# A hybrid attention/retention layer in fp32 on one core: retention values projected with tokens on partitions, rotations in that group, eight heads beside the gates' group

## The chip, the core and the metric

The kernel runs on one core of a Trainium2 chip, in one launch. The metric is device microseconds of that core from launch to end, as the median of several executions. A profile is one more execution, with a time of its own. TensorE (PE in the profile, PEld for its weight loads) makes matrix products into PSUM, eight banks of 128 x 512 fp32; ScalarE (ACT) and VectorE (DVE) read PSUM and SBUF; GpSimd (POOL) reads SBUF; SyncE (SP) issues nearly all DMAs, in order, on one queue.

## The reference

One layer on `x` (1 x 1024 x 2048), fp32: an adaptive RMSNorm, one input projection to eight blocks of 1024 columns, stick-breaking attention on the first four blocks (eight heads of 128), chunkwise retention on the last four (eight heads), one output projection.

```python
mod = jax.nn.silu(c) @ w_ada[layer] + b_ada[layer]
shift, scale, gate = jnp.split(mod, 3, axis=-1)
h = rms_norm(x, norm_gain[layer]) * (1.0 + scale[:, None, :]) + shift[:, None, :]
proj = h @ w_in[layer]
q_sb, k_sb, v_sb, z_sb, q_r, k_r, v_r, z_r = jnp.split(proj, split_at, axis=-1)
...
qr = rotary(split_heads(q_r, RET_HEADS))
kr = rotary(split_heads(k_r, RET_HEADS)) * (HEAD_DIM ** -0.5)
vr = split_heads(v_r, RET_HEADS).astype(jnp.float32)
ob = head_group_norm(chunkwise_retention(qr, kr, vr), ret_norm_gain[layer])
ob = ob * jax.nn.silu(z_r.astype(jnp.float32))
y = jnp.concatenate([oa, ob], axis=-1).astype(x.dtype) @ w_out[layer]
x = x + (gate[:, None, :] * y).astype(x.dtype)
```

`rotary` turns the two halves of the 128 channels against each other: `[t1*cos - t2*sin, t1*sin + t2*cos]`. Retention goes in chunks of 128 tokens: a masked product of queries and keys times the values within a chunk, plus the decayed query times a state that each chunk updates from its keys and values.

## The kernel before

**Products.** An fp32 product is three fp32r matmuls (`mm3`, L183 to L186): each operand is cut into a high part (ScalarE, L171) and a low part (VectorE, L173), and high x high, high x low and low x high are added in PSUM. The input projection is done in groups. A group takes four pairs of 128 columns (`q` = 0 to 3) and forms them by a Strassen-like scheme of seven products (`ORDER`) in place of eight; each product has 8 entries (two halves `hh` of the contraction, four `q`), each entry 12 matmuls of 128x128 against 128x512 into the bank of its `q` (`run_entry`, L464). So a group is 56 entries, 672 matmuls. The weights are the stationary operand, the activations the moving one: the output stands with channels on partitions and tokens along the row.

**Groups.** Group 0 starts while the norm's factors are made; groups 0 to 3 hold the attention's q, k, z and v, groups 4 and 5 the retention's keys and values of four heads each (`rk`, `rv`), group 6 (`LAST`) the retention's gates. The retention's queries were made ahead and lie in `rqraw`. Then follows the output projection (`y` in the profile), 56 steps in the same scheme.

**Transfers.** `pump` (L261) keeps two supplies full, within shares of 92 slots of 128 x 512: the raw weights (`A`, 32 loads a group, rows of 512 bytes) and the *ring* of activation factors (`B11`, `T4` and so on, 112 loads a group), each asked for as slots come free. Finished halves go from `c` tiles to DRAM (`pr_rk`, `pr_rv`), by `final` in `evac` (L392).

**Order.** All engines get their instructions in the order in which the code writes them. Each entry calls `tick` twice, so a tick is six matmuls. A tick writes what `later(n, ...)` has put to it, lets one waiting task take a step, and one weight sum. Tasks are generators; what they yield is the number of ticks until their next step. The low halves of weights are cut `LOOK` = 3 entries ahead.

**Retention heads.** `ret_heads` (L1530) is such a task. It starts when head 7 of the attention is done, in group 5. For each head `ret_prepare` (L1342) loads half by half keys and queries, each with a copy whose upper and lower 64 channels are swapped (`sw`), rotates them on VectorE nine ticks later (three instructions a half, L1356 to L1361), and loads the values. `ret_attention` (L1377) then writes a head's work in four steps with `RT_GAP` = 6 ticks between: `turn_k` (transposes of the keys), `values_in` (transposes of the values, L1391 to L1396, two sets of four, each with a ScalarE copy back), `scores`, `states`, `values`, and the normalization, whose last transposes (`finish`) fall into the next head. A head's mask `dm` is loaded when the head starts. Heads 0 to 2 and the start of head 3 run in group 5, the others in group 6 and in the first eight steps of the output projection; at its step 16 all that is left of the tasks is written out (`while tasks: tick()`).

Of the kernel before, what the change touches and what calls it, by code (L numbers as in the profile page):

```python
# [11 lines left out]
F32 = mybir.dt.float32  # L12
# [5 lines left out]
P = 128  # L18
S = 1024
# [4 lines left out]
NH = 8  # L24
# [7 lines left out]
TURN = 2  # L32
RT_GAP = 6
NZ = 7
# [62 lines left out]
def layer_kernel(ctx, tc, x, c, w_ada, b_ada, norm_gain, w_in, sb_q_gain, sb_k_gain, ret_norm_gain, w_out,  # L97
# [17 lines left out]
    rqraw = [dr.tile([P, S], F32, name=f"rqraw{h}") for h in range(NH)]  # L115
    proj = {f"{n}{h}": dr.tile([P, S], F32, name=f"pr_{n}{h}") for n in ("q", "k", "z", "v", "rk", "rv")
            for h in range(NH)}
    krow = [dr.tile([1, S], F32, name=f"krow{h}") for h in range(NH)]
    sums_o = {(n, k): dr.tile([P, S], F32, name=f"sum_{n}_{k}") for n in ("T2", "T3") for k in range(8)}
# [263 lines left out]
    def evac(gi, prod, q, o):  # L383
# [79 lines left out]
    def run_entry(j):  # L463
# [11 lines left out]
        for k in range(4):  # L475
# [7 lines left out]
            if k % 2:  # L483
                tick()


# [854 lines left out]

    def ret_prepare(h):  # L1342

        r = {}

        def load(n, src, hf):
            r[n, hf] = t = get(f"r{n}_{h}_{hf}", "att")
            nc.sync.dma_start(t, src[:, halves(hf)])
# [5 lines left out]
            def rotate():  # L1354
# [6 lines left out]
                nc.vector.tensor_tensor(t, t, sw, op=ALU.add)  # L1361
                put(sw)
            later(9, rotate)

        def load_v():
            for g in range(2):
                r["v", g] = t = get(f"rv_{h}_{g}", "att")
                nc.sync.dma_start(t, proj[f"rv{h}"][:, halves(g)])

        load("k", proj[f"rk{h}"], 0)  # L1370
        later(2, lambda: load("q", rqraw[h], 0))
        later(4, load_v)
        later(6, lambda: load("k", proj[f"rk{h}"], 1))
        later(8, lambda: load("q", rqraw[h], 1))
        return r

    def ret_attention(h, r, gap):  # L1377
# [10 lines left out]
        def four(t):  # L1388
            return t.rearrange("p (j n) -> p j n", n=P)

        def values_in(g, t):  # L1391
            tp = ps.tile([P, HALF], F32, tag=next_bank(), name=f"rvt_{h}_{g}")
            for j in range(4):
                nc.tensor.transpose(tp[:, j * P:(j + 1) * P], t[:, j * P:(j + 1) * P], ident)
            v[g] = t
            later(1, lambda: nc.scalar.activation(t, tp, AF.Copy))  # L1396

# [107 lines left out]

        vr = [r["v", g] for g in range(2)]
        if unfinished:
            unfinished.pop()()
        turn_k(0)
        values_in(0, vr[0])  # L1510
        scores(0)
        yield gap
        turn_k(1)
        states(0)
        scores(1)
        yield gap
        values_in(1, vr[1])
        values(0)
# [11 lines left out]
    def ret_heads():  # L1530
        while prog.get(NH - 1, 0) < 12 or phase[0] < 5:
            yield 1
        for i, n in enumerate(("cos", "sin")):
            for hf in range(2):
                tables[n, hf] = t = get(f"{n}_{hf}", "att")
                nc.sync.dma_start(t, rot[i][:, halves(hf)])
        nxt = ret_prepare(0)
        yield 14
        while prog[NH - 1] < 99:
            yield 1  # L1540
        for h in range(NH):
            r = nxt
            for i, wait in enumerate(ret_attention(h, r, RT_GAP)):
                if i == 0 and h < NH - 1:
                    while h == 3 and phase[0] < 6:
                        yield 1
                    nxt = ret_prepare(h + 1)
# [5 lines left out]
        put(*tables.values())  # L1553

# [144 lines left out]
    for j in range(len(entries)):  # L1699
        gi, prod, hh, q = entries[j]  # L1700
        if j == 0 or entries[j - 1][0] != gi:
# [5 lines left out]
            if gi == 5:  # L1707
                start(ret_heads(), 3)
            slots.loose = gi == LAST
# [22 lines left out]
        if left_over <= 3:  # L1732
            cut_right(3 - left_over, 0)
        run_entry(j)

# [192 lines left out]
```

## Time and profile before

| | |
|---|---|
| median of 3 runs | 1884.33 us (1883.38 to 1884.34) |
| the profiled execution | 1884.66 us |
| its span, first to last instruction | 1882.9 us |
| PE busy / DVE busy / ACT busy | 1866.6 / 1341.8 / 826.1 us |
| DMA engines' mean share over the span, SyncE's queue | 86.9% |
| group 5 (retention k, v of heads 4 to 7) | 1182 to 1372 us |
| group 6 (retention gates) | 1372 to 1568 us |
| output projection | 1568 us to the end |

How to read it: a matmul's row shows 390 ns, but matmuls overlap, and what one costs is the distance from one start to the next. The share of the DMA engines is the time of all packets over the time of 16 engines; it can pass 1, since a packet's time includes what it waits for. `PEclk` is the granted clock; it is 1.00 in all windows shown.

### The profile page before, as it was taken

The page shows a single profiled execution, that of the slowest core. Times are in us where ns is not written, and L with a number is a line of the kernel's source. Part 1 is how long each engine was busy: PE and PEld are TensorE (multiplying, and loading weights), DVE is VectorE, ACT ScalarE, POOL GpSimd, SP SyncE. Part 2 cuts the span into 40 slices and gives each one's busy share as a digit, 9 for nine tenths or more (in the row PEclk, how much of TensorE's full clock was granted, in tenths as well). Part 3 has the DMA queues.
Part 4 walks back from the last instruction along what each step waited for, and adds up shares of the span by engine and source line. Part 5 has one row for each costly group of instructions (what it writes and reads, how often), then busy time and mean ns, then how long its engine had stood idle before and what let it go on. Part 6 is the DMA issues. An engine that isn't in the chain of part 4 may idle for free.

```text
span 1882.9 us, 29009 instructions
## 1 busy us (share of the span) xinstructions
PE 1866.6 (99%) x9565; PEld 1540.5 (82%) x9565; DVE 1341.8 (71%) x2601; ACT 826.1 (44%) x1559; POOL 82.6 (4%) x278
## 2 busy tenths in 40 slices
PE   8999999999999999999999999999999999999998
PEld 5777788888888888888888888888888888888887
DVE  3568776666768677877688676977585666596669
ACT  3647762233544454445443554334334455342231
POOL 0000000000110010001010101000000000000000
PEclk9999999999999999999999999999999999999999
DMA  9979999998698789978997988999997963994594
GB/s 317 361 240 313 319 348 370 374 359 300 209 315 299 242 285 310 305 272 264 321 317 263 305 276 290 302 304 290 308 317 253 265 214 113 359 366 163 187 313 164
DMA packets 414451, 541.04 MB, mean 287 GB/s; under 512 B 34142, under 2 KB 210648, under 8 KB 414300
## 3 DMA queue, kind: packets, MB, share of 16 engines
q1 hardware_dynamic: 413436, 538.78, 86.9%
q8 instruction: 75, 1.23, 0.3%
q14 instruction: 76, 0.62, 0.1%
q10 hardware_dynamic: 864, 0.40, 0.1%
HBM read 453.03 MB, written 86.02 MB: 286 GB/s over the span
## 4 chain that ended last, share of the span: by engine, by line
PE 92%; DVE 4%; DMA 3%; issue 1%; ACT 0%; SPq 0%; DVEq 0%; ACTq 0%
PE pj L184 19%; PE pj L186 19%; PE pj L185 19%; PE y L185 5%; PE y L184 5%; PE y L186 5%; PE first L184 3%; PE first L186 2%; PE first L185 2%; PE accp L569 1%; PE tp_B L1248 1%; PE oT L184 1%; PE oT L186 1%; PE oT L185 1%; DMA ada<-in_w_ada_dram 1%; PE zp L186 1%
## 5 line engine op out<-in xcount | busy, mean ns | idle before, releaser
L173 DVE TENSOR_TENSOR wl<-A,wh 128x512 fp32r<-128x512 f32 x392 | 270.1, 690 | 211.5 <-ACT wh L171 198.1
L171 ACT ACTIVATE wh<-A 128x512 fp32r<-128x512 f32 x392 | 247.6, 632 | 387.0 <-PE pj L185 369.8
L387 ACT ACTIVATE c<-pj 128x512 f32<-128x512 f32 x112 | 66.7, 600 | 147.4 <-PE pj L186 137.4
L294 DVE TENSOR_TENSOR A<-A,A 128x512 f32<-128x512 f32 x160 | 110.0, 693 | 1.7
L390 DVE TENSOR_TENSOR c<-pj,c 128x512 f32<-128x512 f32 x112 | 74.9, 687 | 47.9 <-PE pj L186 47.5
L1212 ACT ACTIVATE om<-zp,y 128x128 f32<-128x128 f32 (+2 forms) x96 | 55.9, 582 | 107.4 <-PE zp L186 67.2
L184 PE MATMUL first<-h_hi,wh_first 128*128 128x512 f32 x224 | 94.6, 422 | 0.1
L1228 DVE TENSOR_TENSOR_SCAN om<-om 128x128 f32<-128x128 f32 (+2 forms) x96 | 93.5, 974 | 1.1
L184 PE MATMUL pj<-T1h,wh 128*128 128x512 f32 x232 | 94.2, 406 | 0.0
L184 PE MATMUL pj<-B22h,wh 128*128 128x512 f32 x232 | 92.8, 400 | 0.0
L184 PE MATMUL pj<-B21h,wh 128*128 128x512 f32 x232 | 92.0, 397 | 0.0
L184 PE MATMUL pj<-B11h,wh 128*128 128x512 f32 x232 | 91.4, 394 | 0.0
L186 PE MATMUL pj<-T1h,wl 128*128 128x512 f32 x232 | 90.7, 391 | 0.0
L186 PE MATMUL pj<-B22h,wl 128*128 128x512 f32 x232 | 90.6, 391 | 0.0
L185 PE MATMUL pj<-T1l,wh 128*128 128x512 f32 x232 | 90.5, 390 | 0.0
L185 PE MATMUL pj<-B21l,wh 128*128 128x512 f32 x232 | 90.5, 390 | 0.0
L186 PE MATMUL pj<-B21h,wl 128*128 128x512 f32 x232 | 90.4, 390 | 0.0
L186 PE MATMUL pj<-B11h,wl 128*128 128x512 f32 x232 | 90.4, 390 | 0.0
L185 PE MATMUL pj<-B11l,wh 128*128 128x512 f32 x232 | 90.4, 390 | 0.0
L185 PE MATMUL pj<-B22l,wh 128*128 128x512 f32 x232 | 90.4, 390 | 0.0
L184 PE MATMUL pj<-T3h,wh 128*128 128x512 f32 x224 | 89.6, 400 | 0.0
L184 PE MATMUL pj<-T4h,wh 128*128 128x512 f32 x224 | 89.5, 400 | 0.0
(411 smaller groups left out, 4963.2 us busy)
## 6 DMA issues: line engine op xcount, KB each, us to landing
A<-in_w_in_dram SPq DMA_DIRECT2D x228, 256.0 KB, 5.7
ada<-in_w_ada_dram SPq DMA_DIRECT2D x120, 256.0 KB, 5.6
wB<-in_w_out_dram SPq DMA_DIRECT2D x112, 256.0 KB, 5.3
gr<-in_w_ada_dram SPq DMA_DIRECT2D x64, 256.0 KB, 5.6
T2h<-fac_T SPq DMA_DIRECT2D x56, 256.0 KB, 5.4
T2l<-fac_T SPq DMA_DIRECT2D x56, 256.0 KB, 5.4
T1h<-fac_T SPq DMA_DIRECT2D x56, 256.0 KB, 5.4
T1l<-fac_T SPq DMA_DIRECT2D x56, 256.0 KB, 5.3
```

The lines of the kernel that those rows point to most:

```text
L171: nc.scalar.activation(hi[:, 0:n], src[:, 0:n], AF.Copy)
L173: nc.vector.tensor_tensor(lo[:, 0:n], src[:, 0:n], hi[:, 0:n].bitcast(F32), op=ALU.subtract)
L184: nc.tensor.matmul(o, a_hi, b_hi, start=first, stop=False, skip_group_check=on)
L185: nc.tensor.matmul(o, a_hi, b_lo, start=False, stop=False, skip_group_check=on)
L186: nc.tensor.matmul(o, a_lo, b_hi, start=False, stop=last, skip_group_check=on)
L294: nc.vector.tensor_tensor(r[o], r[a], r[b], op=ALU.add if n == 1 else ALU.subtract)
L387: nc.scalar.activation(t, o, AF.Copy)
L390: nc.vector.tensor_tensor(dst[q, cc], o, dst[q, cc], op=ALU.add)
L569: nc.tensor.matmul(ap_[32 * g:32 * g + 32, :], silu_z[:, j, :], ada[cc, j // 2][:, (j % 2) * 256:(j % 2) * 256 + 256], start=j < 4, stop=j ...
L1212: nc.scalar.activation(om[:, :n], zp[:, :n], AF.Sigmoid, scale=y[:, 16 + i:17 + i])
L1228: nc.vector.tensor_tensor_scan(rev, rev, rev, init, op0=ALU.mult, op1=ALU.bypass)
L1248: nc.tensor.transpose(banks_[j // 2][:, c0:c0 + P], be[:, j * P:(j + 1) * P], ident)
```

## The change

Group 4 now holds the keys of all eight heads, and group 5 (`ACROSS`) all values, with the operands' roles turned: activations stationary, 512 columns of weights moving (`run_across`), so that tokens stand on partitions, as the head's products need them. The values go to `rvt`. `values_in` with its transposes and copies is gone; `values_in` in `ret_prepare` is now the name of two loads. A new task, `turn_in`, starts with group 5, waits for the same point of attention head 7 as `ret_heads` did, makes all 32 half-rotations, one every three ticks, and stores each to DRAM (`rot_k`, `rot_q`). `ret_heads` is started near the end of group 5, waits for group 6, and runs all heads with `RT_GAP` = 4, loading rotated halves; a guard on `turns` holds a head's loads until its halves are stored. The raw weights of group 5 are loaded as rows of 2 KB.

```diff
-RT_GAP = 6
+RT_GAP = 4
...
+    rvt = {(c_, hf): dr.tile([P, 4, HALF], F32, name=f"rvt_{c_}_{hf}") for c_ in range(2) for hf in range(2)}
+    turned_in = {(n, h): dr.tile([P, S], F32, name=f"rot_{n}{h}") for n in "kq" for h in range(NH)}
...
-    for a in (0, 4):
-        groups.append([(base + b * P, proj[f"{n}{b}"], proj[f"{n}{b + 1}"])
-                       for b in (a, a + 2) for n, base in (("rk", 5 * GW), ("rv", 6 * GW))])
+    groups.append([(5 * GW + a * P, proj[f"rk{a}"], proj[f"rk{a + 1}"]) for a in range(0, NH, 2)])
+    ACROSS = len(groups)
+    groups.append([(6 * GW, None, None)] * 4)
...
+        if gi == ACROSS:
+            kc += q
+            col = groups[gi][q][0] + (HALF if block[1] == "2" else 0)
+            nc.sync.dma_start(t, w_in[0][kc * P:(kc + 1) * P, col:col + HALF])
+            return
...
+            if gi == ACROSS:
+                def out():
+                    nc.sync.dma_start(rvt[int(cc[0]) - 1, hf][:, q, :], t)
+                    put(t)
+                later(2, out)
+                return
...
+    def run_across(j):
+        gi, prod, hh, q = entries[j]
+        prepare_sum(j + LOOK + 2)
+        prepare_sum(j + LOOK + 3)
+        rt = [right(gi, prod, 4 * hh + q + d) for d in range(2)]
+        l = [lefts.pop(j + d) for d in range(2)]
+        fresh, last = hh == 0 and q == 0 and prod in FRESH, hh == 1 and q == 2
+        for t in range(4):
+            if fresh:
+                bank[t] = bank_for(gi, t, prod)
+            sl = slice(t * P, (t + 1) * P)
+            for d in range(2):
+                mm3(bank[t], rt[d][0][:, sl], rt[d][1][:, sl], l[d][0], l[d][1], fresh and d == 0, last and d == 1,
+                    True)
+            if last:
+                later(1, lambda t=t, o=bank[t]: evac(gi, prod, t, o))
+            tick()
+            if t == 0:
+                prepare_entry(j + LOOK)
+        for d in range(2):
+            put(*rt[d])
+        prepare_entry(j + LOOK + 1)
...
+    def turn_in():
+        while prog.get(NH - 1, 0) < 12:
+            yield 1
...
+        def one(n, h, hf):
+            src = proj[f"rk{h}"] if n == "k" else rqraw[h]
+            t = get(f"r{n}_{h}_{hf}", "att")
             nc.sync.dma_start(t, src[:, halves(hf)])
             sw = get(f"sw_{n}{h}_{hf}", "att")
...
+            def back():
+                nc.sync.dma_start(turned_in[n, h][:, halves(hf)], t)
+                put(t)
+                turns[0] += 1
             later(9, rotate)
...
+            later(11, back)
+        for h in range(NH):
+            for n in "kq":
+                for hf in range(2):
+                    one(n, h, hf)
+                    yield 3
...
+        def load(n, hf):
+            r[n, hf] = t = get(f"r{n}_{h}_{hf}", "att")
+            nc.sync.dma_start(t, turned_in[n, h][:, halves(hf)])
+        def load_v(g):
+            r["v", g] = t = get(f"rv_{h}_{g}", "att")
+            nc.sync.dma_start(t.rearrange("p (j n) -> p j n", n=P),
+                              rvt[h // 4, g][:, :, h % 4 * P:(h % 4 + 1) * P])
+        def values_in(n):
+            later(n, lambda: load_v(0))
+            later(n + 1, lambda: load_v(1))
...
-        def values_in(g, t):
-            tp = ps.tile([P, HALF], F32, tag=next_bank(), name=f"rvt_{h}_{g}")
-            for j in range(4):
-                nc.tensor.transpose(tp[:, j * P:(j + 1) * P], t[:, j * P:(j + 1) * P], ident)
-            v[g] = t
-            later(1, lambda: nc.scalar.activation(t, tp, AF.Copy))
...
     def ret_heads():
-        while prog.get(NH - 1, 0) < 12 or phase[0] < 5:
+        nxt, values_in = ret_prepare(0)
+        while phase[0] < 6:
             yield 1
...
+        values_in(3)
+        yield 2
         for h in range(NH):
             r = nxt
             for i, wait in enumerate(ret_attention(h, r, RT_GAP)):
                 if i == 0 and h < NH - 1:
-                    while h == 3 and phase[0] < 6:
+                    while turns[0] < 4 * (h + 2):
                         yield 1
...
             if gi == 5:
-                start(ret_heads(), 3)
+                start(turn_in(), 1)
...
+        if gi == ACROSS and j + 6 < len(entries) and entries[j + 6][0] != ACROSS and entries[j + 5][0] == ACROSS:
+            start(ret_heads(), 1)
+        if gi != ACROSS:
+            run_entry(j)
+        elif q % 2 == 0:
+            run_across(j)
```

Since tasks and ticks set the order, the program's own rows show the move. First SyncE within group 5. Before, while head 0 runs and head 1 is loaded (`gr` gate weights, `T2` ring factors):

```order
L1001 DMA gr_4_13967<-in_w_ada_dram 128x2x256
L1381 DMA dm_13990<-in_ret_mask_dram 128x256
L1348 DMA rk_0_14012<-pr_rk_135 128x512
L1350 DMA sw_k_0_14014<-pr_rk_135 64x512
L1351 DMA sw_k_0_14014<-pr_rk_135 64x512
L1348 DMA rq_0_14043<-rqraw_95 128x512
L1350 DMA sw_q_0_14045<-rqraw_95 64x512
L1351 DMA sw_q_0_14045<-rqraw_95 64x512
L1368 DMA rv_0_14070<-pr_rv_143 128x512
L1368 DMA rv_1_14072<-pr_rv_143 128x512
L271 DMA T2h_4_14074<-fac_T_4_218 128x512
L273 DMA T2l_4_14076<-fac_T_4_218 128x512
```

And after, in the middle of group 5:

```order
L1410 DMA rot_k_150<-rk_0_14516 128x512
L1393 DMA rk_0_14704<-pr_rk_139 128x512
L1395 DMA sw_k_0_14706<-pr_rk_139 64x512
L1396 DMA sw_k_0_14706<-pr_rk_139 64x512
L279 DMA B21h_4_14720<-fac_B_4_198 128x512
L281 DMA B21l_4_14722<-fac_B_4_198 128x512
L279 DMA B21h_5_14724<-fac_B_5_199 128x512
L281 DMA B21l_5_14726<-fac_B_5_199 128x512
L266 DMA A_6_0_1_14728<-in_w_in_dram 128x4x128
L1410 DMA rot_k_150<-rk_1_14567 128x512
L266 DMA A_6_1_1_14741<-in_w_in_dram 128x4x128
L1393 DMA rk_1_14752<-pr_rk_139 128x512
```

The loads of rotated material came in one burst a head; now a half, its two swaps and a store stand between every few ring loads, all through the group.

Second, SyncE after the change where head 0 begins (`c` are finished value halves):

```order
L405 DMA rvt_1_145<-c_5_3_14640 128x512
L405 DMA rvt_0_144<-c_5_3_13938 128x512
L1455 DMA dm_15420<-in_ret_mask_dram 128x256
L1432 DMA rk_0_15437<-rot_k_147 128x512
L1436 DMA rv_0_15446<-rvt_0_142 128x4x128
L1432 DMA rq_0_15451<-rot_q_155 128x512
L1436 DMA rv_1_15465<-rvt_1_143 128x4x128
```

Head 0's mask and values are asked for as the head begins. Before, that held for the mask alone: the values of head 0 stood 17 rows ahead of it.

Third, TensorE at a head's first and second step, before:

```order
L1405 MATMUL ktp_0_13996<-ident,rk_0_13745 128x128 x4
L1394 MATMUL rvt_0_14001<-ident,rv_0_13834 128x128 x4
L1431 MATMUL sp_0_14006<-rq_0_13769,rk_0_13745 128x128 x4
L184 MATMUL pj_1_1_13983<-B11h_2_13626,wh_1_1_0_13875 128x512
L185 MATMUL pj_1_1_13983<-B11l_2_13628,wh_1_1_0_13875 128x512
```

and after, where the first two rows are the first step, the others the second, four ticks on:

```order
L1472 MATMUL ktp_0_15426<-ident,rk_0_15237 128x128 x4
L1498 MATMUL sp_0_15431<-rq_0_15246,rk_0_15237 128x128 x4
...
L1472 MATMUL ktp_1_15501<-ident,rk_1_15292 128x128 x4
L1480 MATMUL up_0_15506<-rv_0_15446,kd_0_15425 128x128 x4
L1498 MATMUL sp_1_15511<-rq_1_15305,rk_1_15292 128x128 x4
```

The value transposes are gone from the first step; `up`, in the second, is the first to read the loaded values.

More of the change, by code (lines that the diff above doesn't have):

```diff
@@ L1362, in rotate, with ret_prepare @@
                 put(sw)
+            def back():
+                nc.sync.dma_start(turned_in[n, h][:, halves(hf)], t)
+                put(t)
+                turns[0] += 1
             later(9, rotate)
[L1365 to L1375, printed above, removed]
+            later(11, back)
+        for h in range(NH):
+            for n in "kq":
+                for hf in range(2):
+                    one(n, h, hf)
+                    yield 3
+        yield 12
+        put(*tables.values())
+    turns = [0]
+    def ret_prepare(h):
+        r = {}
+        def load(n, hf):
[8 more added lines that the diff above has]
+            later(n + 1, lambda: load_v(1))
+        load("k", 0)
+        later(1, lambda: load("q", 0))
+        later(4, lambda: load("k", 1))
+        later(5, lambda: load("q", 1))
+        if h:
+            values_in(3)
+        return r, values_in
     def ret_attention(h, r, gap):
@@ L1504, in values_last @@
             pending.extend((lambda: finish(0), lambda: finish(1)))
-        vr = [r["v", g] for g in range(2)]
         if unfinished:
@@ L1513, in ret_attention @@
         turn_k(1)
+        v.update({g: r["v", g] for g in range(2)})
         states(0)
@@ L1530, in ret_heads @@
     def ret_heads():
-        while prog.get(NH - 1, 0) < 12 or phase[0] < 5:
+        nxt, values_in = ret_prepare(0)
+        while phase[0] < 6:
             yield 1
[L1533 to L1540, printed above, removed]
+        values_in(3)
+        yield 2
         for h in range(NH):
```

15 lines of the change are left out of this document (5 added, 10 removed).

## The prediction, made before the change was run

> **What bounds the kernel now.** I read the page first, then the windows by stage, then the timeline of single queues.
>
> ```profile
> PE 1866.6 (99%) x9565; PEld 1540.5 (82%) x9565; DVE 1341.8 (71%) x2601; ACT 826.1 (44%) x1559; POOL 82.6 (4%) x278
> q1 hardware_dynamic: 413436, 538.78, 86.9%
> PE 92%; DVE 4%; DMA 3%; issue 1%; ACT 0%; SPq 0%; DVEq 0%; ACTq 0%
> ```
>
> TensorE is busy for 1866.6 of 1882.9 us and holds 92% of the chain of waits, so whatever leaves TensorE is saved and whatever makes it wait is lost. One queue, that of SyncE, carries nearly all bytes at a mean of 86.9% of the DMA engines' time. A mean hides where it is full, so the windows come next.
>
> ```profile
> core 0: us, PE busy (x) PEld busy (x) DVE busy (x) ACT busy (x) POOL busy (x), PEclk, DMA share, GB/s
> 250.00:403.00 153.00, 153.00 (x677) 126.73 (x676) 95.44 (x149) 48.92 (x84) 0.00 (x0) 1.00 1.06 364
> 1182.00:1212.00 30.00, 29.47 (x152) 24.71 (x151) 28.22 (x49) 9.69 (x18) 0.00 (x0) 1.00 1.00 305
> 1212.00:1240.00 28.00, 28.00 (x153) 23.96 (x152) 26.79 (x47) 10.14 (x18) 2.78 (x2) 1.00 1.06 331
> 1294.00:1323.00 29.00, 29.00 (x167) 25.25 (x166) 18.62 (x48) 13.30 (x27) 2.59 (x2) 1.00 1.04 306
> 1182.00:1372.00 190.00, 189.47 (x989) 161.52 (x988) 142.41 (x307) 69.77 (x128) 9.26 (x7) 1.00 0.98 305
> 1372.00:1568.00 196.00, 196.00 (x1056) 167.89 (x1055) 137.11 (x324) 88.52 (x161) 11.65 (x9) 1.00 0.77 242
> ```
>
> 1182 to 1372 is group 5, 1372 to 1568 group 6 (the gates). Over all of group 5 the DMA engines stand at a share of 0.98; group 6 has room, at 0.77. The share hardly passes 1.06, and at that share the queue moved 306 to 364 GB/s: 364 with weights and factors and no heads, 331 and 306 where retention heads load. VectorE works 142.4 of group 5's 190 us. So group 5 has three nearly full resources, and TensorE wins because loads are issued early:
>
> ```profile
> 1119.69 0.36 SPq L271 DMA_DIRECT2D T3h<-fac_T  x1
> 1152.57 0.39 PE L184 MATMUL pj<-T3h,wh 128*128 128x512 f32 x1
> 1348.74 0.52 SPq L271 DMA_DIRECT2D T4h<-fac_T  x1
> 1371.67 0.39 PE L184 MATMUL pj<-T4h,wh 128*128 128x512 f32 x1
> ```
>
> A factor is asked for 32.9 us before its first matmul in group 4, and 22.9 us late in group 5. SyncE's queue already falls some 10 us behind there, hidden by that lead.
>
> **Part 1: the value transposes go.**
>
> ```profile
> 1215.95 0.60 PE L1405 MATMUL ktp<-ident,rk 128*128 128x128 f32 x4
> 1216.38 0.60 PE L1394 MATMUL rvt<-ident,rv 128*128 128x128 f32 x4
> 1216.82 1.06 PE L1431 MATMUL sp<-rq,rk 128*128 128x128 f32 x8
> L1396 ACT ACTIVATE rv<-rvt x16: 579/598/600, 1217.2 to 1562.1; 128x512 f32<-128x512 f32 x16
> 1220.01 0.39 PE L185 MATMUL pj<-B11l,wh 128*128 128x512 f32 x1
> 1222.73 0.39 PE L185 MATMUL pj<-B11l,wh 128*128 128x512 f32 x1
> ```
>
> Four transposes start at 1216.38 and what follows at 1216.82, so a set costs 0.44 us; 16 sets (two a head) are 16 x 0.44 = 7.0 us off TensorE. The 16 ScalarE copies of 598 ns (9.6 us) lie beside matmuls and are worth nothing. The projection keeps its count: two entries were 2 x 12 matmuls of 128x512, and one call of `run_across` makes 4 x 6. Only the operands' roles change, and both are 128x128 against 128x512. Twelve such matmuls take 1222.73 - 1220.01 = 2.72 us; a tick of six is 1.36 us. **-7.0 us.**
>
> **Part 2: the rotations move into group 5.** `turn_in` makes 32 half-rotations, one every 3 ticks: 96 ticks, 96 x 1.36 = 131 us of TensorE, in which now no head runs. What SyncE must carry in these 96 ticks, in units of 256 KB (0.262 MB): per half-rotation the half itself, the two swapped pieces of 128 KB, and the new store, 3 units, so 96; factors, 112 a group of 112 ticks, so 96; raw weights 30; gate weights, one each 8 ticks, 11; value stores 10 (the rest follows). That is 243 units, 63.7 MB. In 131 us it needs 487 GB/s. No window above moved over 364.
>
> How long 63.7 MB take is the term that decides. Two ways to price it. By rates: 364 GB/s gives 175 us, 331 gives 192, 306 gives 208. By the spacing of single transfers:
>
> ```profile
> 1203.87 0.32 SPq L1348 DMA_DIRECT2D rk<-pr_rk  x1
> 1204.53 0.45 SPq L1350 DMA_DIRECT2D sw_k<-pr_rk  x1
> 1205.19 0.45 SPq L1351 DMA_DIRECT2D sw_k<-pr_rk  x1
> 1205.86 0.41 SPq L1348 DMA_DIRECT2D rq<-rqraw  x1
> 299.78 0.42 SPq L273 DMA_DIRECT2D T2l<-fac_T  x1
> 303.94 0.32 SPq L271 DMA_DIRECT2D T2h<-fac_T  x1
> DMA to landing us min/median/max: 3.7/5.7/6.3
> ```
>
> The last row is the landing of the query swaps. A half with its two swaps keeps the queue for 1205.86 - 1203.87 = 1.99 us (a swap of 128 KB takes as long as 256 KB elsewhere), and the seven factor loads from 299.78 to 303.94 took 0.59 us each. 32 x 1.99 = 64, and the other 179 units at 0.59 are 106: 170 us. The mix is nearest to the row 1212:1240, where two heads' halves, swaps and factors share the queue, but the stores and many raw loads are of the plain kind; I take 183 us, between the 170 of the spacing and its 192. Ends: 170 and 208. The excess over TensorE is 183 - 131 = 52 us (39 to 77).
>
> The Trainium skill, "DMA: Bandwidth & Descriptors", section "Where 436 GB/s comes from", names two ceilings, 435 GB/s at the SBUF ports and about 358 for one core's share of HBM. The trace's 364 without heads stands at the lower one. By 435 the stretch would take an estimated 146 us and the sum would be 1889; by 358 it would take 178 us and the sum would be 1921.
>
> Does TensorE see the excess? The factors' 23 to 33 us of lead, less 5.7 us landing, would hide 17 to 27 us. The rotations have less: VectorE rotates 9 ticks (12.2 us) after the load is written down, so from 12.2 - 5.7 = 6.5 us of lag on it waits in order, and queued behind it are the low halves of the weights (three entries, 8 us ahead of TensorE) and the bank evacuations (3 ticks, 4.1 us, at a product's end in `run_across`, against three entries before). So TensorE can be some 10 to 12 us ahead of the queue, and not more.
>
> That lead is then given back at group 6's start. In SyncE's rows just before head 0 (the second place shown with the change), the mask `dm` and the values `rv` stand behind all of group 5's transfers. Head 0's mask product is due one tick after `dm`, and its `states(0)` three ticks (4.1 us and small work) after `rv`, against 5.7 us to land. A lag of 10 us becomes a TensorE wait of about 10 us here. So nearly the whole excess is lost; I deduct 3 us for SyncE running ahead when the stretch begins (0 to 10). **+49 us (29 to 77).**
>
> **Part 3: VectorE in the same stretch.**
>
> ```profile
> L173 DVE TENSOR_TENSOR wl<-A,wh 128x512 fp32r<-128x512 f32 x57 | 39.1, 687 | 23.0 <-ACT wh L171 21.3 <-PE pj L185 1.4
> L294 DVE TENSOR_TENSOR A<-A,A 128x512 f32<-128x512 f32 x24 | 17.1, 714 | 0.2
> L1010 DVE SCALAR_TENSOR_TENSOR ga<-gr,silu_c,ga 128x256 f32<-128x256 f32 x25 | 13.1, 523 | 0.5
> L390 DVE TENSOR_TENSOR c<-pj,c 128x512 f32<-128x512 f32 x19 | 12.6, 686 | 6.0 <-PE pj L186 6.0
> L1357 DVE SCALAR_TENSOR_TENSOR rq<-rq,qb,cos 128x512 f32<-128x512 f32 x8 | 6.0, 744 | 0.0
> L1361 DVE TENSOR_TENSOR rk<-rk,sw_k 128x512 f32<-128x512 f32 x8 | 5.5, 692 | 0.3
> L1360 DVE TENSOR_TENSOR rk<-rk,cos 128x512 f32<-128x512 f32 x8 | 5.5, 685 | 0.0
> ```
>
> A key half is 2 x 685 + 692 = 2.06 us, a query half 2 x 744 + 692 = 2.18; 32 halves are 68 us. The rest by 96 of 112 ticks: 48 splits 33, sums (24 of 714 ns and 8 like them) 20, some 14 additions 10, 22 gate steps 12. Sum 143 us against 131: VectorE too is 12 us over. It runs beside the longer transfers, so it adds nothing to 183; if they fit, it is the bound (a rival).
>
> **Part 4: heads every 16 ticks in group 6.** Their rotations are gone (8.5 us of VectorE a head), loads come ready-made, and group 6 had a DMA share of 0.77. All eight heads now fall between its second entry and the output's second half, before the flush at step 16. TensorE's own work there is the same. Each gap shrinks from 6 ticks to 4 (8.2 to 5.4 us); the states need a ScalarE copy and four short VectorE steps in it. I price this at 0, with 0 to 8 us for the range.
>
> **Sum.** The profiled execution took 1884.66 us, 1.8 more than its span; the median is 1884.33. 1884.3 - 7.0 + 49 = **1926 us**. Its own range: 1884.3 - 7 + 29 = 1906 to 1884.3 - 7 + 77 = 1954.
>
> **Rivals.** *The queue hides it (faster).* If the queue kept up, only Part 1 is left: 1877. For it: TensorE waited nowhere in group 5 though the share was 0.98. Against it: 487 GB/s, 34% above the fastest window. Chance 0.08. *VectorE is the bound, the transfers fit in the leads.* The 12 us over, of which up to 8 lie in the splits' lead: 1877 + 4 to 12 = 1881 to 1889. For it: 94 and 96% VectorE in 1182:1240. It decides if the queue moves above 445 GB/s (63.7 MB in 143 us). Chance 0.10. *Worse than the range*: rotated stores wait on SyncE for a late VectorE and drain the queue, or the gaps of Part 4 open; over 1954. Chance 0.07. *The change doesn't do what it says*: the guard on `turns` could hold heads back until the flush, where they would run bare. The order speaks against it: after the change a head's first key transpose stands every 96 projection matmuls, evenly.
>
> **How the numbers follow.** Forecast 0.75, rivals 0.08, 0.10 and 0.07. Range 1888 to 1950: it cuts a little at the forecast's upper end and leaves out the fast rival and most of VectorE's. Some 0.2% (3.8 us) is what a measurement can tell: faster 0.09, same 0.04, slower 0.87.
>
> **What would show it.** Right: `rvt<-ident` gone; in group 5 a DMA share over 1 at 330 to 370 GB/s from start to end, group 5 longer than 200 us where its matmuls and head 7's rest need some 160, VectorE waiting for `rk`, `rq` or `sw` loads, TensorE for `wl` or a bank, one wait of several us for `rv` or behind `dm` at head 0, group 6 free of waits after it. Wrong: group 5 at about 160 us, or the loss sitting in group 6. The forecast fails most simply if 63.7 MB pass faster than any window here shows.

## The result

The changed kernel takes **1945.14 us** (median of 4 runs, 1941.89 to 1946.30) against 1884.03 us before (4 runs, 1883.38 to 1884.34): 1.032 times as long, 95% interval 1.0307 to 1.0332. That is slower by 61 us, where 42 were forecast; it lies inside the forecast's range, 5 us from its upper end. Two single executions, 3963 us in experiment 8 and 8101 us of the kernel before beside experiment 9, are left out of the intervals below.

The profile after comes from an execution of 1946.04 us (span 1944.0, where before had 1882.9). First the page's busy times, granted clock in 40 slices, queue and chain of waits:

```profile
PE 1882.3 (97%) x9501; PEld 1546.4 (80%) x9501; DVE 1340.7 (69%) x2601; ACT 816.6 (42%) x1543; POOL 82.1 (4%) x278
PEclk9999999999999999999999999988889999999999
q1 hardware_dynamic: 416508, 555.57, 85.9%
PE 85%; DMA 9%; DVE 3%; issue 1%; SPq 1%; ACT 0%; ACTq 0%; DVEq 0%
```

TensorE runs 64 matmuls fewer (the 16 sets of value transposes) and yet is busy 15.7 us longer, 1882.3 against 1866.6. The rest of its span, in which it does nothing, grew from 16.3 to 61.7 us. Together that is the 61 us. DMA's share of the chain rose from 3 to 9%, while the queue's mean share fell: the mean doesn't show the loss. The fall of the clock in slices 27 to 30 (48.6 us each, so 1264 to 1458 us) shows where to look, and the windows there (us, busy time of each engine, granted clock, DMA share, GB/s) are:

```profile
core 0: us, PE busy (x) PEld busy (x) DVE busy (x) ACT busy (x) POOL busy (x), PEclk, DMA share, GB/s
1182.00:1212.00 30.00, 29.87 (x155) 25.31 (x154) 26.07 (x45) 9.82 (x19) 0.00 (x0) 1.00 0.99 314
1212.00:1255.00 43.00, 42.98 (x189) 34.92 (x188) 38.45 (x63) 12.13 (x22) 0.00 (x0) 1.00 0.96 299
1255.00:1392.00 137.00, 104.34 (x387) 79.67 (x385) 77.77 (x126) 25.20 (x42) 0.00 (x0) 0.87 1.04 326
1392.00:1426.00 34.00, 20.17 (x79) 16.74 (x80) 17.99 (x31) 3.27 (x5) 2.55 (x2) 0.70 1.05 344
1182.00:1392.00 210.00, 177.20 (x727) 139.89 (x725) 142.29 (x233) 47.15 (x80) 0.00 (x0) 0.92 1.02 319
1426.00:1623.00 197.00, 197.00 (x1109) 170.62 (x1108) 111.31 (x333) 93.25 (x174) 15.53 (x12) 1.00 0.66 221
```

Group 5 now lasts 210 us in place of 190. For 73 us TensorE runs without a wait on the loads that were issued early. From 1255 the DMA share is above 1, and TensorE is idle for 137 - 104.34 = 32.7 us, and for 13.8 more up to 1426. All the idle time that came is in these two rows. From 1426 to the output projection, which starts at 1623, TensorE is never idle and the queue has room (0.66). The view of waits names what TensorE and VectorE waited for between 1182 and 1426 (us in total, times, the longest):

```profile
DVE sw_q L1401 <- DMA sw_q<-rqraw: 33.1, 13, 5.7
DVE sw_k L1404 <- DMA sw_k<-pr_rk: 22.5, 8, 6.6
PE pj L187 <- DVE wl L175: 21.6, 9, 6.8
DVE pT L1503 <- DMA dm<-in_ret_mask_dram: 13.6, 1, 13.6
PE up L1480 <- DMA rv<-rvt: 11.6, 1, 11.6
```

VectorE waits for the swapped halves, the low weights `wl` stand behind it on the same engine, and TensorE waits for them. So the engine named for TensorE, VectorE, was itself waiting for the queue. TensorE's two rows are 33.2 of its 46.5 us; for 7.0 more the view names no releaser, and 6.2 are for the evacuation of a bank. The last row is the single long wait at head 0. In the timeline, SyncE's queue there reads (start us, us of issue, line, transfer):

```profile
1412.88 0.79 SPq L405 DMA_DIRECT2D rvt<-c  x2
1414.23 0.33 SPq L1455 DMA_DIRECT2D dm<-in_ret_mask_dram  x1
1415.36 0.58 SPq L1436 DMA_DIRECT2D rv<-rvt  x1
```

and TensorE's:

```profile
1408.48 0.60 PE L1472 MATMUL ktp<-ident,rk 128*128 128x128 f32 x4
1420.64 2.04 PE L1480 MATMUL up<-rv,kd 128*128 128x128 f32 x8 [11.55 <-DMA rv<-rvt]
```

The values are asked for at 1415.36, 6.9 us after TensorE began its last work before them.

### The profile page after: what moved, and what is told of

Same layout as the page of the kernel before. It is cut to its first block, busy times and chain, and to the rows that moved or that the text cites. A ratio compares the mean times of both kernels' runs of the same rounds, so it can differ in the third digit from the quotient of the medians.

```text
span 1944.0 us, 28991 instructions
## 1 busy us (share of the span) xinstructions
PE 1882.3 (97%) x9501; PEld 1546.4 (80%) x9501; DVE 1340.7 (69%) x2601; ACT 816.6 (42%) x1543; POOL 82.1 (4%) x278
## 4 chain that ended last, share of the span: by engine, by line
PE 85%; DMA 9%; DVE 3%; issue 1%; SPq 1%; ACT 0%; ACTq 0%; DVEq 0%
PE pj L186 17%; PE pj L187 17%; PE pj L188 17%; PE y L188 4%; PE y L186 4%; PE y L187 4%; PE first L186 3%; PE first L188 2%; PE first L187 2%; PE accp L607 1%; DMA sw_k<-pr_rk 1%; DMA A<-in_w_in_dram 1%; PE tp_B L1286 1%; DMA rq<-rqraw 1%; PE oT L186 1%
## 5 line engine op out<-in xcount | busy, mean ns | idle before, releaser
L398 DVE TENSOR_TENSOR c<-pj,c 128x512 f32<-128x512 f32 x112 | 74.5, 687 | 42.4 <-PE pj L188 41.8
L187 PE MATMUL first<-h_lo,wh_first 128*128 128x512 f32 x224 | 88.7, 396 | 0.2 <-DVE h_lo L638 0.2
L188 PE MATMUL first<-h_hi,wl_first 128*128 128x512 f32 x224 | 88.7, 396 | 0.0
L186 PE MATMUL pj<-T1h,wh 128*128 128x512 f32 x200 | 81.5, 408 | 0.0
L186 PE MATMUL pj<-B22h,wh 128*128 128x512 f32 x200 | 80.1, 401 | 0.0
L186 PE MATMUL pj<-B21h,wh 128*128 128x512 f32 x200 | 79.6, 398 | 0.0
L186 PE MATMUL pj<-B11h,wh 128*128 128x512 f32 x200 | 78.8, 394 | 0.0
L188 PE MATMUL pj<-T1h,wl 128*128 128x512 f32 x200 | 78.3, 391 | 0.0
L187 PE MATMUL pj<-T1l,wh 128*128 128x512 f32 x200 | 78.1, 391 | 0.0
L187 PE MATMUL pj<-B21l,wh 128*128 128x512 f32 x200 | 78.0, 390 | 0.0
L187 PE MATMUL pj<-B22l,wh 128*128 128x512 f32 x200 | 78.0, 390 | 0.0
```

Of the source, the lines that this page charges most:

```text
L186: nc.tensor.matmul(o, a_hi, b_hi, start=first, stop=False, skip_group_check=on)
L187: nc.tensor.matmul(o, a_hi, b_lo, start=False, stop=False, skip_group_check=on)
L188: nc.tensor.matmul(o, a_lo, b_hi, start=False, stop=last, skip_group_check=on)
L398: nc.vector.tensor_tensor(dst[q, cc], o, dst[q, cc], op=ALU.add)
```

## The experiments

Times with no interval are one execution each. The first four were measured beside one execution of the kernel before at 1885.95 us; 1945.14 is the change. The change's own four executions lie 4.4 us apart, so a difference of that size between single runs says nothing. Where a few us matter, the median of several is given with its interval.

**1. The swapped halves in one piece.** A swapped half is loaded by two transfers of 64 rows. Here it is one of 128 rows (the rows are then not exchanged); bytes and VectorE's work are the same.

```diff
-            nc.sync.dma_start(sw[0:64, :], src[64:128, halves(hf)])
-            nc.sync.dma_start(sw[64:128, :], src[0:64, halves(hf)])
+            nc.sync.dma_start(sw, src[:, halves(hf)])
```

> Leaves out the swap itself: the second copy of each half is loaded straight, as one transfer of 128 rows, in place of two of 64 rows with upper and lower halves exchanged. Bytes and VectorE's work stay. Theory (SyncE's queue is the bound in group 5, and the 64-row transfers are what is dear in it, 1.99 us for a half with its swaps against 2 x 0.6): 32 x 0.7 = 22 us less, about 1923 us. Rival A (the queue is the bound by bytes alone): 1940 to 1948. Rival B (VectorE is the bound): unchanged, 1940 to 1948.

Measured: **1923.11 us**. The same bytes in half the pieces save 22.0 us, 0.69 us for each of the 32 pieces saved. The window that stood at 326 GB/s now has:

```profile
1255.00:1392.00 137.00, 110.60 (x448) 87.19 (x446) 87.50 (x141) 28.67 (x47) 0.00 (x0) 0.92 1.07 376
```

The share is about the same as in the change (1.04), and the rate is 376. (Group 6 begins at 1371 here; up to there the rate is 377.) The engines are as full with 64-row pieces, but move less. The packets themselves are longer: of the 18165 packets of 2 KB that start in this window of the change, 2809 take 120 ns or more, and here 287 of 21018. Half the packets take 84 ns in both. The 42 pieces issued in the window have 42 x 64 = 2688 packets, so the cost lies in the packets of the pieces and not in the starting of a transfer. The Trainium skill, "SBUF — State Buffer", section "Door 1: The DMA port swizzle (why `[64,N]` ≈ `[32,N]`)", says that a transfer on 64 partitions reaches only 8 of the 16 ports into SBUF, so that its rate is about half of one on 128. The trace agrees: 128 KB took 0.66 us before, and a piece saved is worth 0.69 here, about what 256 KB take at 376 GB/s (0.70).

**2. No swapped halves.** The two loads go, and VectorE multiplies the half itself in their place.

```diff
-            nc.sync.dma_start(sw[0:64, :], src[64:128, halves(hf)])
-            nc.sync.dma_start(sw[64:128, :], src[0:64, halves(hf)])
...
-                    nc.vector.tensor_tensor(sw, sw, sin, op=ALU.mult)
+                    nc.vector.tensor_tensor(sw, t, sin, op=ALU.mult)
```

> Leaves the second copy's loads out; VectorE computes the same three instructions a half from the half itself. 211 units of 256 KB in the stretch in place of 243. Theory (queue): 32 x 1.3 = 42 us less transfer time, about 1900 to 1910 us, group 5 still over 160 us. Rival A (bytes at 325 GB/s): 8.4 MB less, 26 us, about 1919. Rival B (VectorE): 1940 to 1948.

Measured: **1903.38 us**, as the theory said: 41.8 us for 64 pieces of 128 KB, 0.65 us each. The rival that counts bytes (1919) falls.

**3. No arithmetic.** The rotations' VectorE instructions go, all transfers stay.

```diff
-                    nc.vector.scalar_tensor_tensor(sw, sw, qb[:, 1, h:h + 1], sin, op0=ALU.add, op1=ALU.mult)
-                    nc.vector.scalar_tensor_tensor(t, t, qb[:, 0, h:h + 1], cos, op0=ALU.add, op1=ALU.mult)
...
-                nc.vector.tensor_tensor(t, t, sw, op=ALU.add)
```

> Leaves the rotations' three VectorE instructions a half out; all transfers stay. VectorE has 68 us less work in group 5. Theory (queue): the transfers still need some 200 us; TensorE may run 17 to 27 us ahead instead of 10, and gives that back at head 0, whose values come last: 1930 to 1946 us. Rival B (VectorE is the bound): 1877 to 1890 us.

Measured: **1933.99 us**. From 1255 (group 6 begins at 1378 here):

```profile
1255.00:1392.00 137.00, 107.67 (x421) 85.13 (x421) 43.84 (x73) 26.07 (x43) 0.00 (x0) 0.89 1.04 335
```

VectorE has 43.84 us to do in 137, and TensorE still stands idle for 29.3 of them at a DMA share of 1.04. VectorE is not the bound, but its instructions add some 11 us. SyncE's own waits in the change, between 1182 and 1395, show a way (us in total, times, the longest):

```profile
SPq L1410 <- DVE rq L1406: 4.1, 4, 3.2
SPq L1410 <- DVE rk L1406: 4.0, 6, 1.5
```

L1410 is the store of a rotated half. The queue is in order, so while a store waits for VectorE no later load goes out. 6.2 of these 8.1 us lie before 1255, where VectorE is busy for 38.45 of 43 us and the change moves 299 GB/s. Without the arithmetic these two rows are gone, and the same stretch has:

```profile
1212.00:1255.00 43.00, 43.00 (x191) 35.63 (x190) 21.75 (x37) 12.18 (x20) 0.00 (x0) 1.00 1.05 342
```

That the 11 us are these waits and nothing else of VectorE's is not shown; no run keeps the arithmetic and frees the stores.

**4. No turning at all.** `turn_in` isn't started and heads load the halves as they are.

```diff
-                start(turn_in(), 1)
+                turns[0] = 99
...
-            nc.sync.dma_start(t, turned_in[n, h][:, halves(hf)])
+            nc.sync.dma_start(t, (proj[f"rk{h}"] if n == "k" else rqraw[h])[:, halves(hf)])
```

> Leaves all rotations out: no task in group 5, heads load keys and queries as they were projected. What is left of the change is the values' group with tokens on partitions and eight heads at four ticks. Theory: group 5 has no wait, 7.0 us of transposes are gone, heads at four ticks cost 0 to 8 us: 1877 to 1885 us. Rival C (the values' group itself, with 3 ticks for its banks, or the tighter heads, hold TensorE up): 1890 us or more.

Measured: **1880.87 us**. The values' group and the heads every 16 ticks cost next to nothing. Group 5 ends here at 1341 and group 6 at 1558. The windows show what room there is without rotations:

```profile
1182.00:1341.00 159.00, 158.88 (x724) 132.15 (x723) 84.83 (x144) 46.49 (x80) 0.00 (x0) 1.00 0.85 284
1272.00:1302.00 30.00, 30.00 (x134) 24.86 (x133) 11.61 (x21) 10.55 (x19) 0.00 (x0) 1.00 0.27 78
1302.00:1332.00 30.00, 30.00 (x134) 24.85 (x133) 13.09 (x22) 7.59 (x12) 0.00 (x0) 1.00 1.09 356
1332.00:1362.00 30.00, 25.68 (x122) 21.61 (x121) 18.21 (x33) 6.45 (x10) 2.55 (x2) 0.94 1.06 351
1341.00:1558.00 217.00, 212.68 (x1186) 183.93 (x1185) 123.75 (x356) 97.13 (x180) 18.09 (x14) 0.99 0.69 232
```

Group 5 takes 159 us, and TensorE waits for nothing in it. It already takes 0.85 of the queue, which is full at its end (1302:1332) and at the start of group 6 (most of 1332:1362). The room in it is 0.15 x 159 = 24 us, most of it in one stretch from 1272 (0.27); group 6 has 0.31 x 217 = 67 us. The change spends 51 us more than this run in group 5, and 13 more in group 6, in whose first 34 us the long wait at head 0 stands.

The four runs make a ledger: 1880.87 without rotations; +22.5 for 64 units of 256 KB (halves and rotated halves) with VectorE's work on them; +19.7 for the swapped halves in one piece; +22.0 for cutting them in two: 1945.1. For the 22.5 an estimate is at hand: 64 x 0.70 = 45 us (0.262 MB at the 376 GB/s of experiment 1) less the 24 us of room. It leaves VectorE's part out, and no run shows the two apart there.

**5. Half of them later.** One number: a rotation every 6 ticks, so that half lie in group 6.

```diff
                     one(n, h, hf)
-                    yield 3
+                    yield 6
```

> The change with one number changed: a half-rotation every 6 ticks in place of every 3, so that half of the 32 lie in group 5 and half in the gates' group, each still stored and loaded back. Nothing is left out; same bytes, same VectorE work. Theory (a queue that is asked for more than it carries in one stretch, with room in the next): group 5 is asked for about 179 units of 256 KB in place of 243, some 130 to 140 us of transfer in 131, and the gates' group about 0.85 of its span: 1880 to 1900. Rival (the rotations' bytes cost their time wherever they lie): 1935 to 1948. Rival (half of the excess stays, since the queue is full at any rate): 1908 to 1918.

Measured: **1914.33 us** (4 runs; 1.0165 times before, 1.0148 to 1.0182). The theory's 1880 to 1900 missed; the rival by which half of the excess stays is met. Group 5 ends at 1357 here. Its last windows are full as before, and so is the start of group 6, where TensorE waits 14.7 us for head 0's values:

```profile
1302.00:1332.00 30.00, 23.40 (x102) 18.72 (x101) 13.77 (x23) 5.37 (x9) 0.00 (x0) 0.95 1.08 335
1332.00:1362.00 30.00, 25.32 (x95) 20.40 (x96) 17.76 (x30) 5.06 (x8) 0.00 (x0) 0.84 1.08 331
1362.00:1392.00 30.00, 15.34 (x73) 13.22 (x72) 13.39 (x21) 3.66 (x6) 3.01 (x2) 0.75 1.06 342
```

My count had averaged over group 5, while the run without rotations is at a share of 1.09 in 1302:1332, the end of its group 5, with no rotation in it.

**6. All of them on the fly.** The values' group and heads stay, and each head loads its half and swapped half and turns them itself; nothing is stored back.

```diff
-            nc.sync.dma_start(t, turned_in[n, h][:, halves(hf)])
+            nc.sync.dma_start(t, src[:, halves(hf)])
+            sw = get(f"sw_{n}{h}_{hf}", "att")
+            nc.sync.dma_start(sw[0:64, :], src[64:128, halves(hf)])
+            nc.sync.dma_start(sw[64:128, :], src[0:64, halves(hf)])
...
+            later(8, rotate)
```

> The change's values' group and its order of the heads are kept, but each rotation is made again in its head's own preparation: half and swapped half loaded there, three VectorE instructions eight ticks later, no rotated half stored or loaded back. Nothing is left out. Theory (the excess is the transfers of 32 rotations squeezed into one stretch of 131 us; elsewhere the queue has room, its share is 0.64 in the gates' group without rotations): group 5 as in the run without turning, and the gates' group takes the swaps at a share of about 0.9: 1878 to 1895. VectorE would go from 115 us of 200 in that stretch to some 155 to 165, so it should not bind. Rival (the rotations cost some 40 us of transfer time wherever they lie): 1910 to 1925. Rival (with a head every 16 ticks VectorE's queue is the bound in the gates' group): over 1925.

Measured: **1900.00 us** (4 runs; 1.0084, 1.0069 to 1.0099), 5 us above the theory's range and below both rivals. TensorE's long waits after 1300:

```profile
PE up L1496 <- DMA rv<-rvt: 14.1, 1, 14.1
PE y L186 <- DVE c L398: 4.8, 1, 4.8
```

Two places: head 0's loads and the tables fall on the full end of group 5, and the last head's rotations on VectorE delay the evacuations at the edge of the output. Experiment 7 bears this out in part: there the second wait is gone and the first is halved.

**7 and 8. Prepared two heads ahead.** Tables and heads 0 and 1 are loaded and turned in group 5's room, head h+2 when head h begins; in the second kernel head 0 also begins 4 ticks later (the line with 6; the first keeps 2).

```diff
+        yield 60
...
+        made = {0: ret_prepare(0)}
+        yield 12
+        made[1] = ret_prepare(1)
         while phase[0] < 6:
             yield 1
+        made[0][1](3)
-        yield 2
+        yield 6
...
+                    made[h + 1][1](3)
+                    if h < NH - 2:
+                        made[h + 2] = ret_prepare(h + 2)
```

> As the run with the rotations on the fly (values' group kept, a half and its swapped half loaded and turned in the head's own preparation, nothing stored back), but prepared two heads ahead: the tables and heads 0 and 1 are loaded and turned in group 5 some 60 and 72 ticks after the last stick-breaking head, where the queue's share is 0.27 without turning; head h+2 when head h begins. Nothing is left out. Theory (the 14.1 us that the run on the fly waits for rv of head 0 is the lag of 4 tables and 8 rotations' loads put where the queue is full anyway, and its 4.8 us at the edge of the output is VectorE with the last head's rotations): both go, and the wait of 4.3 us that the run without turning has stays: 1880 to 1886. Rival (the loads find no slack, since the queue's idle stretch only shows that its buffers are full, and the lag is at the edge as before): 1895 to 1902.

> The same, with head 0 begun 4 ticks (5.4 us) later behind the request for its values. Nothing is left out. Theory (head 0 waits 4.3 us for rv because it begins before the last rows of the values can have gone out and come back; TensorE has other work in those ticks): the wait goes, 1876 to 1882. Rival (the work that is put off ends later behind the gates' group, where it costs as much): as the run with head 0 begun at once, within 1.5 us.

Measured: **1886.13 us** (10 runs; 1.0009, 0.9999 to 1.0019) and **1882.27 us** (10 runs; 0.9988, 0.9979 to 0.9998). They are 0.1 and 0.3 us above their theories' ranges and outside their rivals'. The first still waits for head 0's values, 7.2 us:

```profile
PE up L1494 <- DMA rv<-rvt: 7.2, 1, 7.2
```

With head 0 begun later that wait is gone, and the loads lie in the room that was there (0.27 without rotations):

```profile
1272.00:1302.00 30.00, 30.00 (x134) 24.85 (x133) 20.46 (x35) 11.15 (x20) 0.00 (x0) 1.00 0.85 241
```

Experiment 8's expectation has head 0 wait for the last rows of the values. The program shows another reason: the rows that head 0 reads were stored a product earlier (experiment 10). What stands just ahead of the request on SyncE's queue are the eight stores for heads 4 to 7 (in experiment 7 from 1341.7 us, the request at 1353.7).

This version is 63 us faster than the change and level with the kernel before: its 2 us lie below the 0.2% that a measurement here can tell.

**9. The mask ahead too.** In that version VectorE stood for 9.97 us at head 0's mask, asked for 5.5 us ahead, and TensorE then waited 2.1 and 1.1 us for state sums queued behind it. On VectorE and on SyncE's queue:

```profile
1362.67 0.69 DVE L1517 TENSOR_TENSOR pT<-sp,dm 128x512 f32<-128x512 f32 x1 [9.97 <-DMA dm<-in_ret_mask_dram]
```

```profile
1357.18 0.34 SPq L1469 DMA_DIRECT2D dm<-in_ret_mask_dram  x1
```

The next kernel loads the mask in `ret_prepare`, and prepares head h+2 at step 2 of head h, not step 0.

```diff
-                if i == 0 and h < NH - 1:
-                    made[h + 1][1](3)
-                    if h < NH - 2:
-                        made[h + 2] = ret_prepare(h + 2)
+                if i == 0 and h < NH - 1:
+                    made[h + 1][1](3)
+                if i == 2 and h < NH - 2:
+                    made[h + 2] = ret_prepare(h + 2)
```

> The run prepared two heads ahead with head 0 begun 4 ticks later, and two changes: a head's mask (dm) is loaded with its preparation, not when the head begins, and head h+2 is prepared 8 ticks after head h began. Nothing is left out. Theory (at head 0 VectorE stood 10 us for dm, loaded 5 us before its use, and TensorE then waited 2.3 and 1.3 us for the state sums queued behind it; nothing else waits over 1 us after the start): both waits go, 1876 to 1880, faster than before by 0.2 to 0.4%. Rival (another load of head 0, its values or halves, is as late as dm, and TensorE waits for that): 1880 to 1884, as the run before it.

Measured: **1885.79 us** (11 runs; 1.0007, 0.9998 to 1.0016), above the theory's range and its rival's. TensorE's waits after 1300:

```profile
PE y L186 <- DVE c L398: 6.1, 2, 3.1
PE up L1495 <- DMA rv<-rvt: 0.6, 1, 0.6
```

Both waits at head 0 went, and two of 3 us came at the edge of the output, where bank evacuations stand behind VectorE as in experiment 6. Which of the two edits brought them was not separated.

**10. Values of head 0 asked for earlier.** In the change.

```diff
         nxt, values_in = ret_prepare(0)
+        values_in(2)
         while phase[0] < 6:
             yield 1
-        values_in(3)
```

> The change with one line moved: the values of head 0 are asked for when the heads begin, some ticks ahead of the gates' group, not at its first ticks. Nothing is left out. Theory (the single long wait of 11.7 us behind rv of head 0 is where the queue's lag is given back, not a cost of its own; the lag has to come back somewhere): the wait goes, another of nearly its size stands at the next load, and the time stays within 4 us of the change's 1944. Rival (the wait at head 0 is a misplaced request): 1930 to 1935.

Measured: **1943.20 us**. The loads, at 1392.8 and 1394.3 us, now stand ahead of the last eight stores of values (from 1404.9). Those are for heads 4 to 7 (`rvt_1_0` and `rvt_1_1`, which product 7 finishes); head 0 reads `rvt_0_0` and `rvt_0_1`, finished by products 2 and 3 and stored by 1378.4. So nothing is left out, as expected. TensorE's longest from 1392 to 1440:

```profile
PE pj L188 <- DVE wl L175: 10.9, 1, 10.9
```

The wait for `rv` is gone and one of its size stands at the next weights. It was the lag of the queue being given back.

**11. TensorE kept busy in the stretch.** 256 transposes of the identity into an unused bank.

```diff
+            if prod in ORDER[3:]:
+                if t == 0:
+                    warm = ps.tile([P, P], F32, tag="C", name=f"warm_{j}")
+                for _ in range(4):
+                    nc.tensor.transpose(warm, ident, ident)
```

> The change with 256 transposes of the identity into an unused bank added on TensorE, four ahead of each tick's matmuls in the last four of group 5's seven products (some 0.11 us each at full clock, 28 us in all); nothing else is changed or left out. They fill TensorE's waits in small pieces, so fewer waits are long enough for the granted clock to fall. Theory (the queue sets that stretch and TensorE's half clock, 51 us of the span, lies inside time that it would wait anyway): 1940 to 1948. Rival (the half clock costs time of its own, 10 to 20 us): 1924 to 1934. Rival (TensorE's own work sets the stretch at the end, and the added transposes come on top): 1955 to 1972.

Measured: **1945.92 us**. In the stretch:

```profile
1255.00:1392.00 137.00, 121.48 (x637) 98.22 (x635) 76.80 (x124) 24.40 (x41) 0.00 (x0) 0.98 1.05 322
```

The granted clock is 0.98 in place of 0.87 and 256 more instructions run, and the time is the same. In group 5 this much of TensorE's clock and of its work is free; the queue sets the time. (The 34 us after it were left as they are.)

**12. Two queues.** `turn_in`'s loads go out on ScalarE's queue.

```diff
-            nc.sync.dma_start(t, src[:, halves(hf)])
+            nc.scalar.dma_start(t, src[:, halves(hf)])
```

(so too the swapped halves and tables.)

> The change with the loads of turn_in (the halves, the swapped halves and the tables) issued on ScalarE's queue, not on SyncE's; the stores stay. Same bytes; nothing is left out. Theory (the 16 DMA engines carry no more than some 325 GB/s of this mixture, whoever asks): 1935 to 1950, the share over 1 in the same stretch. Rival (one queue in order is the bound, by the time of an issue or because loads queue behind what isn't due): 1890 to 1920, and more GB/s in the stretch. A third way: ScalarE's stream waits at loads for buffers and its copies out of the banks come late: over 1955.

Measured: **1947.19 us**, and in the stretch:

```profile
1255.00:1392.00 137.00, 106.47 (x396) 80.15 (x396) 82.74 (x134) 24.03 (x42) 0.00 (x0) 0.90 1.06 319
```

Nearly the same rate (319 against 326 GB/s) at nearly the same share. For these loads it is not the one queue's order but the engines behind it, as the Trainium skill has it in "DMA: Bandwidth & Descriptors", section "Issuing engines are not separate DMA queues": whoever issues, the transfers share the same 16 engines.

## Why the prediction was right, and what it mis-sized

The direction, the mechanism and the places came out as forecast; the forecast of the excess was too small by 15 us, most of it from VectorE, which was priced at nothing. (The runs behind this split are single ones, so a few us either way stay open.)

- **Part 1, -7.0 us.** TensorE's busy time without turning is 1860.1 us, 6.5 below the kernel before. Right.
- **Part 2, the excess.** Forecast 49 us, measured 1945.14 - 1880.87 = 64.3. SyncE issues the load of the first half at 1193.6 us and of the last at 1388.0: 31 of 32 steps in 194 us, so 201 us for all, where 183 were taken. Group 5 moved 319 GB/s, which makes 64 MB in 201 us: the 63.7 MB were right, the time for them was not. Two steps failed. The first is "the other 179 units at 0.59 are 106". The 0.59 us are the spacing of seven issues and not what the engines carried: 0.262 MB in 0.59 us are 444 GB/s, above every window, and in those 4.16 us of the kernel before the engines moved 293 at a share of 0.90. The swapped pieces were priced well (0.66 us, measured 0.65 to 0.69). With the 64-row pieces gone the mixture moved 376 GB/s, which is 0.70 us for 0.262 MB; 179 x 0.11 = 20 more on the spacing's 170 give an estimate of 190 for the queue alone. The run without arithmetic, with the same transfers, has its halves from 1192.4 to 1377.5: 191 us. The window 1212:1240 of before, at 192, was the better guide.
- **Part 3, the second step.** VectorE's 143 us are not the bound (experiment 3). But "it adds nothing to 183" failed: with VectorE's instructions the stretch takes 201 us and not 191, and the kernel 11 us longer, and SyncE's stores wait 8.1 us for VectorE in it. The prediction named such waits among its rivals, for times over 1954. Of the 64.3 us, 53.1 are left without the arithmetic (1933.99 - 1880.87), near the 49 of the queue alone.
- **How the excess reaches TensorE.** VectorE late for the swapped halves, TensorE for `wl`, and the lead given back at head 0 in one wait (forecast 10 us, 11.6 measured) with `dm` and `rv` asked for behind all of group 5: as forecast. Experiment 10 shows that this wait is the lag and no cost of its own.
- **Part 4, priced 0 (0 to 8).** Without turning the time is 3.6 us above the 1877.3 that Part 1 alone gives; the one new wait there is 4.3 us for head 0's values.
- **The sum.** 1884.3 - 7.0 + 3.6 + 64.3 = 1945.2. It closes by construction, since the last two terms are differences between the runs.
- **The page's two ceilings** (the Trainium skill, "DMA: Bandwidth & Descriptors", section "Where 436 GB/s comes from"). Neither decided: with 64-row pieces the stretch moved 319 GB/s (326 from 1255 on), below both, and without them 376, above the lower one of 358.

## What to carry to other kernels

Price a moved stage by the room of the resource in the very stretch it moves into, window by window: a queue at 0.85 over 159 us was full at the end where it counted. Take the price of a transfer from what a window with the same mixture moved, not from the spacing of a few issues, and count pieces of 64 rows as whole ones. A store on an in-order queue makes every later load wait for the engine that fills it. A round trip through memory that saves another engine nothing is only traffic: here the same rotations, loaded a head or two earlier where the queue had room, cost nothing that could be measured against the kernel before.

## What the hardware showed unexpectedly

Behind waits of some us TensorE's granted clock halved: from 1420.5 to 1425.5, right after the wait of 11.55 us, it is 0.50. In the change's timeline, at 1400 us the matmuls of 128x512 start 0.43 us apart, at 1407 us 0.22:

```profile
1400.34 0.63 PE L187 MATMUL pj<-T4l,wh 128*128 128x512 f32 x1
1400.77 0.63 PE L188 MATMUL pj<-T4h,wl 128*128 128x512 f32 x1
...
1407.34 0.39 PE L187 MATMUL pj<-T4l,wh 128*128 128x512 f32 x1
1407.56 0.39 PE L188 MATMUL pj<-T4h,wl 128*128 128x512 f32 x1
```

A busy time that grew by 15.7 us with 64 instructions fewer is this, and no new work: the run without rotations has the same 9501 instructions, a mean clock of 0.998 in place of 0.984, and 1860.1 us. The Trainium skill, "TensorE: Matmul & The Clock Gate", section "Part 1: The HAM clock gate (the "warmup" mystery)", has two clocks only, whole and half, the half after an idle window of about 3.4 us. The trace agrees: the spacing is whole or half, and between 1272 and 1426 us its record of the clock has ten stretches at 0.50, each 3.4, 6.8 or 13.7 us long, 55 us in all. What experiment 11 adds: it costs nothing as long as another resource sets the time.
